# Scores in 384-column matmuls, summed on VectorE, and the attention projection kept in DRAM

## The chip, the cores and the metric

The kernel runs on one core of a Trainium2 chip. The metric is the device time of one execution in microseconds. Engines are called by their names in the profile: PE is TensorE (PEld its weight loads), DVE is VectorE, ACT is ScalarE, POOL is GpSimd, SP is SyncE, which here issues the DMAs.

## What is computed

One decoder block over 2048 positions of width 1024. After an RMSNorm, one projection gives the inputs of two branches and their gates: a convolution branch (gated input, 31 taps per channel, LayerNorm, SiLU) and a sliding-window attention branch. Both are multiplied by a gate, projected, merged by sigmoid gates, projected once more and added to the input; a final RMSNorm follows. The part that the change touches:

```
qb = q.reshape(B, nb, BLOCK, N_KV_HEADS, GROUP, HEAD_DIM)        # BLOCK 128, GROUP 4, HEAD_DIM 64
kb, vb = band(k), band(v)                                        # the block before and this one
scores = einsum("bnqhgd,bnkhd->bnhgqk", qb, kb) * HEAD_DIM ** -0.5
scores = where(in_window & (key_pos >= 0), scores, -1e30)        # WINDOW 128
m = max(max(scores), sink);  p = exp(scores - m)
probs = p / (sum(p) + exp(sink - m));  out = probs @ vb
y_attn = (out * silu(attn_gate)) @ w_attn_out
merged = g_conv * y_conv + g_attn * y_attn
```

All inputs and the output are float32.

## The kernel before

Positions are worked in two sweeps of 1024. Matrices lie with channels on the 128 partitions; a product is made of three matmuls of 512 columns in float32r, high x high, high x low and low x high parts, 24 matmuls for an output tile of 128 channels by 512 positions (a half). A sweep runs through a list of items in a fixed order: queries and keys with their rotation (`mm_q_a`, `mm_q_b`, `mm_ka`, `mm_kb`), values (`mm_v`), the four sets of gates (`mm_ag`, `mm_cg`, `mm_ma`, `mm_mc`), with the convolution's inputs (`mm_gb`, `mm_ga`) strewn between them, then the attention projection (`mm_ya`), the convolution projection (`mm_yc`) and the output projection (`o`).

PE's order is the order of the program. The class `Line` writes that order: it keeps a clock `t` that advances by 0.6825 us per product (`3 * MM_US`, MM_US = 0.2275), and after each product it starts what is due. Background operations (`bg`, among them the convolution's taps, one `scalar_tensor_tensor` of 128x1024 on DVE each, L536) are let out one per `every` microseconds. Chains are generators; a chain's `yield a, b` says that its step took `a` us of PE and that the next step is due `b` us later. Entries of `soon` go out one per product. Operations wrapped in `od(...)` keep the program's order on their engine.

Attention is a chain, one per unit: 8 blocks of 128 queries by 4 key heads in a sweep, 32 units, started every ATT_EVERY = 13.8 us on the line's clock. A unit makes the scores of its four query heads in four groups, each 64 queries of two heads against 192 keys (L799), copies them out of PSUM into the buffer `ss` (ACT L811, DVE L816), takes the maximum with the sink (DVE L819), the exponentials (ACT L822), the reciprocal of the sum (DVE L825) and the scaling (ACT L828). After LAT[0] it transposes the probabilities (`tpp`, L834), splits them (ACT L842, DVE L259), and after LAT[1] multiplies them with the values (`ov`, L858), adds, gates and stores them (ACT L865, DVE L868 and L869, ACT L872, store L881). In a score matmul the 128 partitions hold the high and low parts of a query side by side against the same key rows; `k` has for every 64 keys their high part and their low part (index j), and the two are accumulated in PSUM by two matmuls.

PSUM has three pools: three `mm` banks for halves, three `tp` banks for scores, transposes and values, and one accumulator of two banks for the convolution. `ss` has four buffers, `pt` and `pc` two each. `t2k` is a set of five SBUF buffers of 128x512, used for gates on their way to and from DRAM and by the LayerNorm.

When the last tap is done, the LayerNorm runs as a chain: mean (`lnmu`), centering, variance (`lnvar`, which takes two `mm` banks), `rstd` (ACT L965), then the normalised channels; after that `u_op` multiplies them with their gate into `uT`, which `mm_yc` reads. Results of `mm_ya` are kept in SBUF tiles `mp` (L1053), six of which take the place of convolution results, and are read by L1076 when `mm_yc` gives the other branch's results.

Of the kernel before, what the change touches and what calls it, by code (L numbers as in the profile page):

```python
# [12 lines left out]
F32 = mybir.dt.float32  # L13
# [6 lines left out]
P = 128  # L20
# [9 lines left out]
HD = 64  # L30
# [13 lines left out]
LN_SUB = 2.6  # L44
GLU_AFTER = (0, 6, 12, 16, 19, 22, 25, 28)
ROPE_EVERY = 3.2
CONV_EVERY = 2.4
ATT_EVERY = 13.8
LAT = (19.0, 13.5)
PRIO = 60  # L50
SCALE = HD ** -0.5


@with_exitstack
def hybrid_block(ctx: ExitStack, tc: tile.TileContext, x, xt, par_d, w_in, w_conv, sinks, w_attn, w_out,
# [70 lines left out]
    for u in range(2):  # L126
        us = slice(u * HD, (u + 1) * HD)
        pool.tensor_copy(out=tri[us], in_=causal[us, us])
    tri_i = tri.bitcast(I32).unsqueeze(1).broadcast_to([P, 2, HD])
    eps = const.tile([P, 2], F32, name="eps_t")  # L130
    dve.memset(eps, EPS)
    act.activation(out=eps[:, 1:2], in_=eps[:, 0:1], func=AF.Sqrt)
# [27 lines left out]
    d_q = dram.tile([P, 2, 2, S // HD, 2, P], F32, name="d_q")  # L160
    d_k = dram.tile([P, 2, 2, S // HD, 2, HD], F32, name="d_k")

    d_a = dram.tile([NSWEEP * NKV, P, 2, 2, T], F32, name="d_a")
    d_v = dram.tile([S // P, P, 2, NKV, P], F32, name="d_v")
    v_halo = const.tile([P, NKV, 2, HD], F32R, name="v_halo")
# [82 lines left out]
    def od(op):  # L248

        tc.stamp_issue_order_token(op.ins, "chain")  # L250
        return op
# [261 lines left out]
    def sweep(s):  # L513
# [270 lines left out]
        def attention(n):  # L784
            g, b = divmod(n, NB)
            begun.add(n)
            u = f"{s}_{g}_{b}"
            blk = s * NB + b
            first = blk == 0
            q, k = qk.pop(n)  # L790
            load_qk(n + 1)
            scs = []
            for qh in range(2):
                scs.append(tp_ps.tile([P, 2, 2 * P], F32, tag="tp", name=f"sc{u}_{qh}"))
                c0 = (P - HD * qh) if first else 0
                for hp in range(2):
                    w = q[:, 2 * qh + hp, :]
                    for j in range(2):
                        pe.matmul(out=scs[qh][:, hp, c0:3 * HD], lhsT=w,  # L799
                                  rhs=k[:, qh + c0 // HD:qh + 3, j, :], start=(j == 0), stop=(j == 1))  # L800
            ss = slot(next_of("ss", AT[4:7] + AT[13:14]), [P, 1024], F32, f"ss{u}")
            sx = ss[:, 0:4 * (P + 4)].rearrange("p (h q) -> p h q", q=P + 4)
            sb, ext = sx[:, :, 0:P], sx[:, :, 0:P + 1]
            oT = ss[:, 768:1024].rearrange("p (a q) -> p a q", q=P)
            pool.tensor_copy(out=sx[:, :, P], in_=sink_bc[:, g * GQ:(g + 1) * GQ])
            if first:
                pool.memset(sb, NEG)
            parts = [sb[:, 2 * qh:2 * qh + 2, :] for qh in range(2)]
            for qh, part in enumerate(parts):
                if not first:  # L810
                    od(act.copy(part, scs[qh][:, :, 0:P]))  # L811
                elif qh:
                    od(act.copy(part[:, :, HD:], scs[qh][:, :, HD:P]))
            yield 0.90, 0.8
            for part, sc in zip(parts, scs):
                od(dve.copy_predicated(out=part[:, :, 0:HD], mask=tri_i, data=sc[:, :, P:3 * HD]))  # L816
            st = work.tile([P, 3, GQ], F32, tag="st", name=f"st{u}", bufs=4)
            ngm, den, rinv = (st[:, i, :] for i in range(3))
            od(dve.tensor_reduce(out=ngm, in_=ext, axis=AX.X, op=ALU.max, negate=True))  # L819
            yield 0.0, 1.2  # L820
            for h in range(GQ):
                od(act.activation(out=ext[:, h, :], in_=ext[:, h, :], func=AF.Exp, bias=ngm[:, h:h + 1],  # L822
                                  accum_out=den[:, h:h + 1]))
            yield 0.0, 3.3
            od(dve.reciprocal(out=rinv, in_=den))  # L825
            yield 0.0, 0.6
            for h in range(GQ):
                od(act.activation(out=sb[:, h, :], in_=sb[:, h, :], func=AF.Copy, scale=rinv[:, h:h + 1]))  # L828
            soft.add(n)
            yield 0.0, LAT[0] - 5.9  # L830

            tpp = tp_ps.tile([P, GQ, P], F32, tag="tp", name=f"tpp{u}")
            for h in range(GQ):
                pe.transpose(out=tpp[:, h, :], in_=sb[:, h, :], identity=ident)  # L834
            e2 = slice(s * KC + 2 * g, s * KC + 2 * g + 2)
            qs = slice(b * P, (b + 1) * P)
            pcg = slot(next_of("pc", AT[9:11]), [P, 1024], F32R, f"pc{u}")
            pc, ga = pcg[:, 0:TH], f(pcg[:, TH:TH + 2 * P]).rearrange("p (a q) -> p a q", q=P)
            nc.sync.dma_start(out=ga, in_=spill["ag"][e2, :, qs].rearrange("c p q -> p c q"))
            pt = slot(next_of("pt", AT[7:9]), [P, 2, TH], F32R, f"pt{u}")  # L840
            flat = tpp.rearrange("p h q -> p (h q)")
            od(act.copy(pt[:, 0], flat))  # L842
            yield 0.44, 0.5
            od(split_lo(pt[:, 1], flat, pt[:, 0], dve))
            for a in range(2):
                at = slice(a * HD, (a + 1) * HD)
                pool.affine_select(out=pc[at], in_=f(pt[0:HD, a]), pattern=[[0, 2 * GQ], [1, HD]],  # L847
                                   compare_op=ALU.is_ge, fill=0.0, base=0, channel_multiplier=-1)
            yield 0.0, LAT[1] - 0.5

            ov = tp_ps.tile([P, TH], F32, tag="tp", name=f"ov{u}")
            mix, da, db = (t[:, n // 4 % 2, b % 4, :] for t in vg[0])
            for qh in range(2):
                cols = slice(qh * 2 * P, (qh + 1) * 2 * P)
                seq = [] if first and not qh else [((v_of(g, b - 1), mix)[qh], pt[:, a, cols]) for a in range(2)]
                seq.append(((da, db)[qh], pc[:, cols]))
                for i, (vv, pp) in enumerate(seq):
                    pe.matmul(out=ov[:, cols], lhsT=vv, rhs=pp, start=(i == 0), stop=(i == len(seq) - 1))  # L858
            if n % 4 == 3 and n // 4 + 2 < 2 * NKV:
                line.after(4.0, reload(n // 4 + 2), lambda: True)  # L860
            ovp = ov.rearrange("p (q i r t) -> p i r q t", q=2, i=2, r=2)
            rows = ((slice(0, HD), slice(HD, P)), (slice(HD, P), slice(0, HD)))
            to = [oT[own].rearrange("p i (q t) -> p i q t", t=HD) for own, _ in rows]
            for r in range(2):
                od(act.copy(to[r], ovp[rows[r][1], :, r]))  # L865
            yield 0.72, 0.6
            for r in range(2):
                od(dve.tensor_tensor(out=to[r], in0=ovp[rows[r][0], :, r], in1=to[r], op=ALU.add))  # L868
            od(dve.tensor_tensor(out=oT, in0=oT, in1=ga, op=ALU.mult))  # L869
            yield 0.0, 1.6  # L870
            hl = sb.rearrange("p (l c) q -> p l c q", c=2)
            od(act.copy(hl[:, 0].bitcast(F32R), oT))  # L872
            yield 0.0, 0.5
            od(split_lo(hl[:, 1].bitcast(F32R), oT, hl[:, 0], dve))
            if n == NKV * NB - 1 and s + 1 < NSWEEP:
                pool.tensor_copy(out=v_halo, in_=f(vt[NB // 2 - 1][:, 1]).rearrange(
                    "p g (a d) -> p g a d", d=HD))
            yield 0.0, 1.0

            def store():  # L880
                nc.sync.dma_start(out=d_a[s * NKV + g, :, :, :, qs], in_=hl)  # L881
                done[n] = True

            line.soon.append(store)
# [156 lines left out]
            flat += todo  # L1041


        mp = {}
        mp_tags = [X[2], X[0]] + C[0:6]

        def ya_item(e, first):
            def ev(half, ps):
                if half == 0:
                    if e > 1:  # L1050
                        line.until(lambda: ("u", e - 2, 1) in stored)
                    mp[e] = slot(mp_tags[e], [P, T], F32, f"mp{s}_{e}")
                act.copy(mp[e][:, half * TH:(half + 1) * TH], ps)  # L1053

            prefetch, blocks, _ = project(w_attn[e], lambda k, half: aT[half][k],
                                       f"ya{s}_{e}", ev)
            if not first:
                return prefetch, blocks

            def first_blocks():  # L1060
                start_u()
                if None in aT[0] + aT[1]:
                    line.finish()
                yield from blocks()

            return prefetch, first_blocks
# [4 lines left out]
        def yc_item(e):  # L1071
            def ev(half, ps):
                if not mT:
                    mT.extend(make_tiles(AT, h, f"mT{s}_") for h in range(2))
                ga, g = (load_gate(kind, AF.Sigmoid, e, half) for kind in ("ma", "mc"))
                dve.tensor_tensor(out=ga, in0=mp[e][:, half * TH:(half + 1) * TH], in1=ga, op=ALU.mult)  # L1076
                dve.tensor_tensor(out=g, in0=ps, in1=g, op=ALU.mult)
                pool.tensor_tensor(out=g, in0=g, in1=ga, op=ALU.add)
                put_split(mT[half][e], g, dve)
# [199 lines left out]
```

## Time and profile before

| | us |
|---|---|
| median of the runs (1990.48 to 1991.02) | 1990.72 |
| profiled execution, whole time | 1991.83 |
| its span, first to last instruction | 1990.1 |
| PE busy in the span | 1975.1 |
| DVE busy | 1318.3 |
| ACT busy | 1000.5 |
| POOL busy | 431.8 |

The attention units of the first sweep lie between 210 and 680 us of the span, those of the second between 1197 and 1670; `mm_ya` and `mm_yc` lie from 734 to 911 and from 1722 to 1896. In the rows of groups the columns are: line, engine, operation, written<-read tiles, shapes, count, then busy us, mean ns of one, and the engine's idle time before them with what ended it. In the rows of the timeline: start us, us, engine, line, operation, count, and in brackets the idle time before. In the chain of waits: start us, us, what. In the rows by stretch: the stretch, its length, busy us and count of PE, PEld, DVE, ACT and POOL, the granted clock, the DMA share and GB/s. Rows on waits: who, for whom, total us, times, longest us.

### The profile page before, as it was taken

What the parts mean: (1) busy time and instruction counts of PE and PEld (TensorE: products, weight loads), DVE (VectorE), ACT (ScalarE), POOL (GpSimd) and SP (SyncE); (2) the same over time, 40 slices, a digit from 0 to 9 for tenths busy, and PEclk for the clock granted to TensorE, in tenths of its full rate; (3) what the DMA queues carried; (4) which work ended last, traced back from release to release, by engine and by line L of the source; (5) the groups of instructions that cost most, each with busy time, mean ns of one, the idle gap of its engine ahead of it and who ended that gap; (6) DMA issues with size and microseconds to landing.
All of it is one profiled execution on the core that took longest, in us unless ns stands there. A gap on an engine that the chain in (4) does not pass through costs nothing.

```text
span 1990.1 us, 27077 instructions
## 1 busy us (share of the span) xinstructions
PE 1975.1 (99%) x9256; PEld 1648.4 (83%) x9256; DVE 1318.3 (66%) x1745; ACT 1000.5 (50%) x2270; POOL 431.8 (22%) x462
## 2 busy tenths in 40 slices
PE   8999999999999999999999999999999999999998
PEld 7888888888888878888888888888888888888887
DVE  6998478987887647143858656787787776432424
ACT  7322567556555457344513126776565555553422
POOL 0445323333333332341001121101101110001200
PEclk9999999999999999999999999999999999999999
DMA  8557746665556855456647575555655678553632
GB/s 309 187 185 221 241 156 197 196 194 182 196 192 217 260 184 169 133 195 248 211 134 247 162 240 174 188 184 180 199 181 171 216 228 265 168 189 133 216 123 85
DMA packets 287548, 386.15 MB, mean 194 GB/s; under 512 B 22961, under 2 KB 138033, under 8 KB 287409
## 3 DMA queue, kind: packets, MB, share of 16 engines
q1 hardware_dynamic: 287408, 384.41, 58.8%
q8 instruction: 73, 1.20, 0.2%
q14 instruction: 67, 0.54, 0.1%
HBM read 252.20 MB, written 132.12 MB: 193 GB/s over the span
## 4 chain that ended last, share of the span: by engine, by line
PE 85%; DVE 2%; ACT 1%; issue 1%; DMA 1%; POOL 0%; SPq 0%; DVEq 0%; POOLq 0%; ACTq 0%
PE mm_cg L302 9%; PE mm_ma L302 9%; PE o L1201 9%; PE mm_yc L302 9%; PE mm_ya L302 8%; PE mm_mc L302 8%; PE mm_ga L302 7%; PE mm_gb L302 7%; PE mm_ag L302 7%; PE sc L799 3%; PE mm_q_b L302 2%; PE mm_q_a L302 2%; PE ov L858 2%; PE tpp L834 1%; PE mm_v L302 1%
## 5 line engine op out<-in xcount | busy, mean ns | idle before, releaser
L536 DVE SCALAR_TENSOR_TENSOR acc<-glu,par,acc 128x1024 f32<-128x1024 f32 x464 | 595.5, 1283 | 6.8
L1201 PE MATMUL o<-wo,mT 128*128 128x512 f32 x768 | 174.8, 389 | 0.0
L1201 PEld LDWEIGHTS o<-wo,mT 128*128 128x128 f32 x768 | 144.1, 188 | 30.0
L302 PE MATMUL mm_ya<-aT,whi_ya 128*128 128x512 f32 x512 | 157.9, 389 | 2.2 <-ACT rstd L965 2.2
L302 PE MATMUL mm_cg<-hT,whi_cg 128*128 128x512 f32 x512 | 159.8, 393 | 0.0
L302 PE MATMUL mm_ma<-hT,whi_ma 128*128 128x512 f32 x512 | 159.7, 393 | 0.0
L302 PE MATMUL mm_ag<-hT,whi_ag 128*128 128x512 f32 x512 | 159.5, 393 | 0.0
L302 PE MATMUL mm_mc<-hT,whi_mc 128*128 128x512 f32 x512 | 158.3, 390 | 0.0
L302 PE MATMUL mm_yc<-uT,whi_yc 128*128 128x512 f32 x512 | 157.6, 389 | 0.0
L302 PE MATMUL mm_ga<-hT,whi_ga 128*128 128x512 f32 x448 | 139.4, 392 | 0.0
L302 PE MATMUL mm_gb<-hT,whi_gb 128*128 128x512 f32 x448 | 139.3, 392 | 0.0
L822 ACT ACTIVATE ss<-ss,st 128x129 f32<-128x129 f32 x256 | 100.1, 394 | 65.9 <-DVE st L819 65.6
L847 POOL TENSOR_SCALAR_AFFINE_SELECT pc<-pt 64x512 fp32r<-64x512 f32 x128 | 83.6, 653 | 206.2 <-ACT pt L842 178.5
L302 PEld LDWEIGHTS mm_ya<-aT,whi_ya 128*128 128x128 f32 x512 | 96.0, 188 | 22.5 <-ACT rstd L965 2.6
L302 PEld LDWEIGHTS mm_yc<-uT,whi_yc 128*128 128x128 f32 x512 | 96.1, 188 | 20.0
L302 PEld LDWEIGHTS mm_mc<-hT,whi_mc 128*128 128x128 f32 x512 | 95.4, 188 | 19.7 <-ACT mu L953 0.3
L302 PEld LDWEIGHTS mm_ag<-hT,whi_ag 128*128 128x128 f32 x512 | 93.6, 188 | 17.8
L302 PEld LDWEIGHTS mm_cg<-hT,whi_cg 128*128 128x128 f32 x512 | 93.3, 188 | 17.4
L259 DVE TENSOR_TENSOR pt<-tpp,pt 128x512 fp32r<-128x512 f32 x64 | 44.2, 691 | 95.7 <-ACT pt L842 95.3
L302 PEld LDWEIGHTS mm_ma<-hT,whi_ma 128*128 128x128 f32 x512 | 93.1, 188 | 17.2
L302 PE MATMUL mm_ma<-hT,wlo_ma 128*128 128x512 f32 x256 | 100.0, 391 | 0.0
L302 PE MATMUL mm_cg<-hT,wlo_cg 128*128 128x512 f32 x256 | 100.0, 390 | 0.0
(452 smaller groups left out, 4274.5 us busy)
## 6 DMA issues: line engine op xcount, KB each, us to landing
qk<-d_q SPq DMA_DIRECT2D x64, 256.0 KB, 4.3
d_a<-ss SPq DMA_DIRECT2D x64, 256.0 KB, 2.8
aT<-d_a SPq DMA_DIRECT2D x32, 512.0 KB, 5.6
qk<-d_k SPq DMA_DIRECT2D x60, 256.0 KB, 4.5
d_k<-hlk SPq DMA_DIRECT2D x16, 512.0 KB, 4.6
d_q<-hq_c SPq DMA_DIRECT2D x16, 512.0 KB, 4.6
raw_ag<-in_w_in_dram SPq DMA_DIRECT2D x32, 256.0 KB, 4.2
d_ag<-ag SPq DMA_DIRECT2D x32, 256.0 KB, 2.9
```

Source lines behind the costliest of these rows:

```text
L259: return eng.tensor_tensor(out=out_, in0=full, in1=f(hi), op=ALU.subtract)
L302: pe.matmul(out=ps, lhsT=a, rhs=b, start=(k == 0 and i == 0), stop=(k == KC - 1 and i == 2))
L536: od(dve.scalar_tensor_tensor(out=to, in0=glu[c][:, j:j + T], scalar=tap(c, j), in1=acc[c], op0=ALU.mult, op1=ALU.add))
L799: pe.matmul(out=scs[qh][:, hp, c0:3 * HD], lhsT=w, rhs=k[:, qh + c0 // HD:qh + 3, j, :], start=(j == 0), stop=(j == 1))
L822: od(act.activation(out=ext[:, h, :], in_=ext[:, h, :], func=AF.Exp, bias=ngm[:, h:h + 1], accum_out=den[:, h:h + 1]))
L834: pe.transpose(out=tpp[:, h, :], in_=sb[:, h, :], identity=ident)
L847: pool.affine_select(out=pc[at], in_=f(pt[0:HD, a]), pattern=[[0, 2 * GQ], [1, HD]], compare_op=ALU.is_ge, fill=0.0, base=0, channel_multi ...
L858: pe.matmul(out=ov[:, cols], lhsT=vv, rhs=pp, start=(i == 0), stop=(i == len(seq) - 1))
L1201: pe.matmul(out=ps, lhsT=a[:, c0:c0 + P], rhs=r, start=(k == 0 and i == 0), stop=(k == KC - 1 and i == 2))
```

## The change

The two matmuls that accumulated a group's scores against the high and the low keys become one matmul of 2 x 192 columns, whose two halves lie side by side in one bank. ACT copies the low half into the score buffer, DVE adds the high half to it, and the mask is applied from that buffer. A unit's scores are made in two steps, the second about SCORE_GAP after the first. The sink's column moves to the front of the buffer. Delays of the line change (CONV_EVERY, LAT[1], the waits around the softmax). Results of the attention projection go into a `t2k` buffer and from there to DRAM (`d_mp`); they are loaded again for L1076, and the evacuation no longer asks for a `u` to have been issued.

```
--- before.py
+++ after.py
@@ -44,11 +44,13 @@
 LN_SUB = 2.6
 GLU_AFTER = (0, 6, 12, 16, 19, 22, 25, 28)
 ROPE_EVERY = 3.2
-CONV_EVERY = 2.4
+CONV_EVERY = 2.5
 ATT_EVERY = 13.8
-LAT = (19.0, 13.5)
+LAT = (19.0, 18.5)
+SCORE_GAP = 3.2
 PRIO = 60
 SCALE = HD ** -0.5
+SW = 1 + 3 * HD
 
 
 @with_exitstack
@@ -126,7 +128,7 @@
     for u in range(2):
         us = slice(u * HD, (u + 1) * HD)
         pool.tensor_copy(out=tri[us], in_=causal[us, us])
-    tri_i = tri.bitcast(I32).unsqueeze(1).broadcast_to([P, 2, HD])
+    tri_i = tri.bitcast(I32).unsqueeze(1).broadcast_to([P, GQ, HD])
     eps = const.tile([P, 2], F32, name="eps_t")
     dve.memset(eps, EPS)
     act.activation(out=eps[:, 1:2], in_=eps[:, 0:1], func=AF.Sqrt)
@@ -160,6 +162,7 @@
     d_q = dram.tile([P, 2, 2, S // HD, 2, P], F32, name="d_q")
     d_k = dram.tile([P, 2, 2, S // HD, 2, HD], F32, name="d_k")
 
+    d_mp = dram.tile([NSWEEP * KC, P, T], F32, name="d_mp")
     d_a = dram.tile([NSWEEP * NKV, P, 2, 2, T], F32, name="d_a")
     d_v = dram.tile([S // P, P, 2, NKV, P], F32, name="d_v")
     v_halo = const.tile([P, NKV, 2, HD], F32R, name="v_halo")
@@ -789,35 +792,36 @@
             first = blk == 0
             q, k = qk.pop(n)
             load_qk(n + 1)
-            scs = []
-            for qh in range(2):
-                scs.append(tp_ps.tile([P, 2, 2 * P], F32, tag="tp", name=f"sc{u}_{qh}"))
-                c0 = (P - HD * qh) if first else 0
-                for hp in range(2):
-                    w = q[:, 2 * qh + hp, :]
-                    for j in range(2):
-                        pe.matmul(out=scs[qh][:, hp, c0:3 * HD], lhsT=w,
-                                  rhs=k[:, qh + c0 // HD:qh + 3, j, :], start=(j == 0), stop=(j == 1))
             ss = slot(next_of("ss", AT[4:7] + AT[13:14]), [P, 1024], F32, f"ss{u}")
-            sx = ss[:, 0:4 * (P + 4)].rearrange("p (h q) -> p h q", q=P + 4)
-            sb, ext = sx[:, :, 0:P], sx[:, :, 0:P + 1]
+            sx = ss[:, 0:GQ * SW].rearrange("p (h q) -> p h q", q=SW)
+            ext, sb = sx[:, :, 0:P + 1], sx[:, :, 1:P + 1]
             oT = ss[:, 768:1024].rearrange("p (a q) -> p a q", q=P)
-            pool.tensor_copy(out=sx[:, :, P], in_=sink_bc[:, g * GQ:(g + 1) * GQ])
+            pool.tensor_copy(out=sx[:, :, 0], in_=sink_bc[:, g * GQ:(g + 1) * GQ])
             if first:
                 pool.memset(sb, NEG)
-            parts = [sb[:, 2 * qh:2 * qh + 2, :] for qh in range(2)]
-            for qh, part in enumerate(parts):
-                if not first:
-                    od(act.copy(part, scs[qh][:, :, 0:P]))
-                elif qh:
-                    od(act.copy(part[:, :, HD:], scs[qh][:, :, HD:P]))
-            yield 0.90, 0.8
-            for part, sc in zip(parts, scs):
-                od(dve.copy_predicated(out=part[:, :, 0:HD], mask=tri_i, data=sc[:, :, P:3 * HD]))
+            for qh in range(2):
+                c0 = (P - HD * qh) if first else 0
+                banks = []
+                for hp in range(2):
+                    sc = tp_ps.tile([P, 4, P], F32, tag="tp", name=f"sc{u}_{qh}{hp}")
+                    sc = sc.rearrange("p a b -> p (a b)").rearrange("p (j c) -> p j c", j=2)
+                    pe.matmul(out=sc[:, :, c0:3 * HD].rearrange("p j (b t) -> p j b t", t=HD),
+                              lhsT=q[:, 2 * qh + hp, :],
+                              rhs=k[:, qh + c0 // HD:qh + 3].rearrange("p b j t -> p j b t"),
+                              start=True, stop=True)
+                    banks.append(sc)
+                to = [sx[:, 2 * qh + hp, 1 + c0:1 + 3 * HD] for hp in range(2)]
+                for part, sc in zip(to, banks):
+                    od(act.copy(part, sc[:, 1, c0:3 * HD]))
+                yield 0.35, 0.5
+                for part, sc in zip(to, banks):
+                    od(dve.tensor_tensor(out=part, in0=sc[:, 0, c0:3 * HD], in1=part, op=ALU.add))
+                yield 0.0, 0.0 if qh else SCORE_GAP - 0.85
+            od(dve.copy_predicated(out=sb[:, :, 0:HD], mask=tri_i, data=sx[:, :, P + 1:]))
             st = work.tile([P, 3, GQ], F32, tag="st", name=f"st{u}", bufs=4)
             ngm, den, rinv = (st[:, i, :] for i in range(3))
             od(dve.tensor_reduce(out=ngm, in_=ext, axis=AX.X, op=ALU.max, negate=True))
-            yield 0.0, 1.2
+            yield 0.0, 2.6
             for h in range(GQ):
                 od(act.activation(out=ext[:, h, :], in_=ext[:, h, :], func=AF.Exp, bias=ngm[:, h:h + 1],
                                   accum_out=den[:, h:h + 1]))
@@ -827,7 +831,7 @@
             for h in range(GQ):
                 od(act.activation(out=sb[:, h, :], in_=sb[:, h, :], func=AF.Copy, scale=rinv[:, h:h + 1]))
             soft.add(n)
-            yield 0.0, LAT[0] - 5.9
+            yield 0.0, LAT[0] - SCORE_GAP - 7.35
 
             tpp = tp_ps.tile([P, GQ, P], F32, tag="tp", name=f"tpp{u}")
             for h in range(GQ):
@@ -1041,16 +1045,13 @@
             flat += todo
 
 
-        mp = {}
-        mp_tags = [X[2], X[0]] + C[0:6]
 
         def ya_item(e, first):
             def ev(half, ps):
-                if half == 0:
-                    if e > 1:
-                        line.until(lambda: ("u", e - 2, 1) in stored)
-                    mp[e] = slot(mp_tags[e], [P, T], F32, f"mp{s}_{e}")
-                act.copy(mp[e][:, half * TH:(half + 1) * TH], ps)
+                m = t2k(f"mp{s}_{e}_{half}")
+                act.copy(m, ps)
+                line.soon.append(lambda: nc.sync.dma_start(
+                    out=d_mp[s * KC + e, :, half * TH:(half + 1) * TH], in_=m))
 
             prefetch, blocks, _ = project(w_attn[e], lambda k, half: aT[half][k],
                                        f"ya{s}_{e}", ev)
@@ -1073,7 +1074,9 @@
                 if not mT:
                     mT.extend(make_tiles(AT, h, f"mT{s}_") for h in range(2))
                 ga, g = (load_gate(kind, AF.Sigmoid, e, half) for kind in ("ma", "mc"))
-                dve.tensor_tensor(out=ga, in0=mp[e][:, half * TH:(half + 1) * TH], in1=ga, op=ALU.mult)
+                m = t2k(f"lmp{s}_{e}_{half}")
+                nc.sync.dma_start(out=m, in_=d_mp[s * KC + e, :, half * TH:(half + 1) * TH])
+                dve.tensor_tensor(out=ga, in0=m, in1=ga, op=ALU.mult)
                 dve.tensor_tensor(out=g, in0=ps, in1=g, op=ALU.mult)
                 pool.tensor_tensor(out=g, in0=g, in1=ga, op=ALU.add)
                 put_split(mT[half][e], g, dve)
```

## The prediction

> **What bounds the kernel now.** I read the page first (span, busy shares), then who PE waited for, then the chain of waits in two places.
>
> ```profile
> span 1990.1 us, 27077 instructions
> PE 1975.1 (99%) x9256; PEld 1648.4 (83%) x9256; DVE 1318.3 (66%) x1745; ACT 1000.5 (50%) x2270; POOL 431.8 (22%) x462
> PE mm_gb L302 <- ACT u_c L377: 5.5, 1, 5.5
> PE mm_ya L302 <- ACT rstd L965: 2.2, 1, 2.2
> PE mm_q_b L302 <- DVE ra_q__0_1573 L614: 0.4, 1, 0.4
> PE sc L799 <- DVE pt L259: 0.2, 1, 0.2
> ```
>
> PE is busy through 99% of the span, and its four listed waits add up to 8.3 us, 5.5 of them at the start, which the change doesn't touch. So time is won by a shorter matmul stream, and lost where PE, whose order is fixed by hand, meets an operand or a PSUM bank that isn't ready. What a matmul costs is its place in that stream:
>
> ```profile
> 187.35 10.88 PE mm_ag L302 x48
> 209.79 0.84 PE sc L799 x8
> 1224.91 0.87 PE sc L799 x8
> 1232.63 0.44 PE tpp L834 x4
> 1235.14 0.71 PE ov L858 x6
> ```
>
> A 512-column matmul takes 10.88/48 = 0.2267 us, one of 256 columns (ov) 0.71/6 = 0.118, one of 128 (tpp) 0.110, and one of 192 (sc) 0.87/8 = 0.109. Below about 256 columns the price no longer falls: a score matmul of 192 columns pays for almost 256.
>
> **1. Eight score matmuls become four of 384 columns.** On the line from 256 to 512 columns, 384 take 0.172 us; four take 0.69 instead of 0.87, so 0.18 us per unit. For 60 units that is 10.8 us. The four units at the sequence's start (0.84 us now) go to two of 128 and two of 256 columns, 0.46 us: 1.5 us more. Together **-12.3 us**, all on PE, hence on the path. Bounds: the operand is read in six pieces of 64 columns, and no row has such a read above the floor. At worst 384 columns cost two of 192 (0.218) and only the 1.5 us stay. I take 0.172, since the 192-column read, already in three pieces, is no dearer than the contiguous 128.
> [...]
>
> **2. More evacuation, on engines that are not the bound.**
>
> ```profile
> L868 DVE TENSOR_TENSOR ss<-ov,ss 64x256 f32<-64x256 f32 x128 | 53.9, 421 | 63.0 <-ACT ss L865 59.1 <-PE mm_gb L302 2.5
> L259 DVE TENSOR_TENSOR pt<-tpp,pt 128x512 fp32r<-128x512 f32 x64 | 44.2, 691 | 95.7 <-ACT pt L842 95.3
> L816 DVE COPY_PREDICATED ss<-tri,sc 128x128 f32<-128x128 int32 x128 | 33.0, 298 | 23.7 <-PE sc L799 10.8 <-ACT ss L811 9.9 <-ACT ss L813 1.4
> L536 DVE SCALAR_TENSOR_TENSOR acc<-glu,par,acc 128x1024 f32<-128x1024 f32 x464 | 595.5, 1283 | 6.8
> L811 ACT COPY ss<-sc 128x256 f32<-128x256 f32 x120 | 43.2, 373 | 45.3 <-PE sc L799 41.8 <-DMA wlo_ma<-d_lo 0.4
> L842 ACT CAST pt<-tpp 128x512 fp32r<-128x512 f32 x64 | 37.4, 585 | 32.9 <-PE tpp L834 32.5
> 230.00:650.00 420.00, 419.77 (x2111) 354.96 (x2110) 338.58 (x456) 256.29 (x690) 145.03 (x172) 1.00 0.60 191
> 1190.00:1640.00 450.00, 450.00 (x2257) 380.68 (x2257) 345.96 (x475) 279.06 (x731) 60.73 (x100) 1.00 0.60 192
> ```
>
> DVE: an addition of 192 columns lies on the line through 256 (421 ns) and 512 (691): 353 ns. Four additions and one predicated copy of 256 elements (about 433, from 298 at 128 and the same slope) are 1.85 us, where two predicated copies took 0.60: +1.25 us a unit. A tap of the convolution every 2.5 instead of 2.4 us gives back 0.23 taps of 1283 ns, 0.29 us. Net +0.96 us in the 13.7 us of a unit, 7 points: DVE goes from 338.58/420 = 81% to 88% in the first sweep's attention, from 77% to 84% in the second's. ACT: four copies of 192 columns (320 ns on the line from 373 to 585) for two of 256: +0.53 us, 61% to 65%. Neither becomes the bound by its sum; what it costs is delay, next.
>
> **3. Banks: six a unit instead of four, on three.** The tp banks serve the scores, the transposes (tpp) and the values (ov). In the new order the fourth score matmul reuses the bank of the first, so PE waits there until the first addition is done. The line's clock advances 0.6825 us per product (three matmuls of MM_US) and starts a step at the first product past its due time: additions are issued 1.03 us after the unit begins (0.35 + 0.68), the second pair of matmuls at 3.76 (0.35 + five products). So the first addition must end 3.9 us after the unit's start. Today's predicated copy is issued at 2.27 (0.90 + two products). When does DVE get there?
>
> ```profile
> 264.27 1.03 PE L799 MATMUL sc<-qk 128*128 128x192 f32 x8
> 268.93 0.49 DVE L816 COPY_PREDICATED ss<-tri,sc 128x128 f32<-128x128 int32 x2
> 319.69 1.00 PE L799 MATMUL sc<-qk 128*128 128x64 f32 x8
> 325.97 0.50 DVE L816 COPY_PREDICATED ss<-tri,sc 128x128 f32<-128x128 int32 x2
> 361.64 0.81 PE L799 MATMUL sc<-qk 128*128 128x192 f32 x6
> 366.75 0.50 DVE L816 COPY_PREDICATED ss<-tri,sc 128x128 f32<-128x128 int32 x2
> 1224.75 1.03 PE L799 MATMUL sc<-qk 128*128 128x192 f32 x8
> 1226.27 0.49 DVE L816 COPY_PREDICATED ss<-tri,sc 128x128 f32<-128x128 int32 x2
> ```
>
> In the ordinary unit (1224.75) DVE starts 1.52 us after the matmuls: a first addition would end near 1.9 at the latest, two microseconds early. But for some nine units of the first sweep (264 to 375) DVE is 4.66, 6.28 and 5.11 us late. The addition stands 1.24 us earlier in DVE's order, which is half a tap, 0.64 us; with its own 0.35 it ends at 4.37, 5.99 and 4.82, that is 0.44, 2.06 and 0.89 us past the 3.9. A PE wait delays all that follows, so a steady lag is paid once: 2 us is the low end. Paid anew by each of nine units at the mean of the first and last, 0.67, it is 6, and with the 0.96 us of part 2 making the lag grow again up to 12. I take **+5 us**, the nearer end being 6, and nothing in the second sweep, where units have two microseconds.
>
> **4. Longer latencies.** The maximum over the scores is issued 4.79 us into the unit instead of 2.27; the waits up to tpp sum to 19.0 us instead of 19.9, so the softmax loses some 3 us of cover and tpp keeps its place. LAT[1] then adds 5 us up to ov: a unit holds its score buffer, one of four, about 4 us longer.
>
> ```profile
> 1267.85 0.52 SPq L881 DMA_DIRECT2D d_a<-ss  x1
> d_a<-ss SPq DMA_DIRECT2D x64, 256.0 KB, 2.8
> 1280.90 0.70 ACT L811 COPY ss<-sc 128x256 f32<-128x256 f32 x2
> ```
>
> The unit of 1224.75 stores at 1267.85, lands at about 1270.7, and its buffer is written by the fourth unit after at 1280.90: 10 us of cover, 6 left. Zero. If that goes, ACT's copy comes late and adds to part 3.
>
> **5. The convolution ends later.** From 210 us to the end of the taps near 676 there are some 195 of them at 2.4 us; 0.1 us more each puts the LayerNorm about 20 us back, in each sweep.
>
> ```profile
> 737.21 0.63 PE L920 MATMUL lnvar<-vsump,ones 128*128 128x512 f32 x2
> 741.33 1.27 ACT L965 ACTIVATE rstd<-lnvar,eps_t 128x512 f32<-128x512 f32 x2
> L259 DVE TENSOR_TENSOR uT<-lcg,uT x16: 676/684/1786, 762.5 to 791.1; 128x512 fp32r<-128x512 f32 x16
> 823.96 87.04 PE mm_yc L302 x384
> 1714.45 0.47 PE lnvar L920 x2
> 1722.44 87.04 PE mm_ya L302 x384
> ```
>
> On today's clock uT would be done near 811 and is first read at 823.96: covered by 12 us. lnvar takes two of the three mm banks; today that costs the 2.2 us of the second wait above, because ACT came 4.1 us late. In the second sweep it moves from before mm_ya (1714.45) into it. Between 0 and 4.1 us in each sweep, 2.2 in all today: I take no change, by that nearest row; the ends are a gain of 2.2 and a loss of 6.
>
> **6. Projection through DRAM.** The evacuation (ACT, L1053) stays, into a t2k buffer; 32 stores and 32 loads of 256 KB come onto SP's queue, and L1076 waits for one more load. The wait of the evacuation for u goes, and was no PE wait.
>
> ```profile
> SPq L596 <- POOL lmc L1078: 20.6, 13, 4.8
> lma<-d_ma SPq DMA_DIRECT2D x32, 256.0 KB, 3.3
> 856.64 0.69 DVE L1077 TENSOR_TENSOR lmc<-mm_yc,lmc 128x512 f32<-128x512 f32 x1 [0.96 <-PE mm_yc L302]
> 862.08 0.69 DVE L1077 TENSOR_TENSOR lmc<-mm_yc,lmc 128x512 f32<-128x512 f32 x1 [0.20 <-PE mm_yc L302]
> ```
>
> A half of mm_yc takes 5.44 us and uses three of the five t2k buffers instead of two. Already now the gate loads wait for buffers (first line). The third load goes out when L1076 has freed its buffer of the half before: 0.69 + 3.3 = 4.0 us a half, under 5.44, so DVE still waits for PE. The new stores stand on SP until ACT's copy is done, as those of the gates do; queued behind a blocked load or store are the weights' loads, a block (10.9 us) ahead. Zero: even a loop of 6 us would lose 0.56 x 16 = 9 us a sweep, inside the two spare mm banks. POOL's copy of the sinks only changes its column.
>
> **Sum.** 1990.1 - 12.3 + 5 = 1982.8 us of span. The profiled execution took 1991.83 in all, 1.73 outside its span and 1.1 over the runs' median of 1990.72; the same -7.3 on that median is **1983 us**.
>
> **Rivals.**
> - No wait worth naming: DVE's lag in those nine units comes from today's spacing (tpp and ov side by side), which LAT spreads out. 1990.7 - 12.3 = 1978.4. For it: the second sweep, no unit late. Chance 0.25.
> - Slower: the bank of the first score. If DVE, at 88%, lags through the first sweep as it does in the nine units, 32 waits of 0.67 cost 21 us: 2000. It decides once the mean wait over 64 units passes 0.19 us, the gain per unit. Against it: 12% of DVE still free, and PE waited 0.2 us for such a bank so far. Chance 0.15. [...]
> - mm banks: lnvar inside mm_ya in both sweeps, 4.1 us each less today's 2.2: 1983 + 6 = 1989, the same. Chance 0.11.
> - 384 columns at 0.218: the change does nothing for PE. 1990.7 - 1.5 + 5 = 1994. Against it: the 512-column price. Chance 0.07.
>
> **How the numbers follow.** The forecast (1979.5 to 1986.5 by its waits of 2 to 8 us) has 0.42. Anything within 0.2% (4 us) can't be told from no change. Faster: 0.42 + 0.25 = 0.67; same: 0.11, most of the fourth rival and a milder bank wait, 0.17; slower 0.16. The range runs from just below the case without waits, 1977, to past the fourth rival, 1995, and leaves out most of the bank rival.
>
> **What would show it.** sc: 256 matmuls, four in 0.69 us of chain. PE's waits: the second pair of scores on DVE's addition, a few microseconds, between 264 and 375 us only. DVE near 88% and 84% in the attention stages. lnvar about 15 us later on the clock. L1077 still waiting for mm_yc. Wrong if sc waits in both sweeps, if four scores take 0.87, or if mm_ya or mm_yc waits for t2k evacuations.

## The result, and the profile after

The changed kernel took 2010.03 us (median; 2009.11 to 2014.66), the kernel before 1990.87 on the same chip: a ratio of 1.0099, interval 1.0081 to 1.0116. It is slower by 1%; the forecast was 1983, the range 1977 to 1995. The profiled execution took 2014.66 in all, some 5 us over the other three, with a span of 2013.0; the stages below are those of that execution, so they show 22.9 us of loss in the span where the medians show 19.2.

First the page of the changed kernel and its list of PE's waits. The change moves line numbers: L1079, L1080 and L1081 are now the two multiplications and the addition of `mm_yc` (L1076 to L1078 before), L1078 the new load, L808 the scores, L818 the new addition, L262 the split of results on DVE, L599 the loads of gates.

```profile
span 2013.0 us, 26940 instructions
PE 1975.2 (98%) x9000; PEld 1637.7 (81%) x9000; DVE 1375.4 (68%) x1937; ACT 1019.6 (51%) x2396; POOL 430.2 (21%) x462
```
```profile
PE mm_yc L305 <- DVE lmc L1080: 12.4, 6, 4.0
PE o L1204 <- ACT wo L1149: 6.6, 3, 4.1
PE mm_gb L305 <- ACT u_c L380: 5.9, 1, 5.9
PE mm_ga L305 <- ACT glu L562: 2.2, 1, 2.2
PE o L1204 <- DVE lmc L1080: 1.8, 1, 1.8
PE o L1204 <- DVE wo L262: 1.1, 3, 0.6
PE sc L808 <- DVE ss L818: 0.3, 1, 0.3
```

The waits that the forecast looked for are missing: 0.3 us for a bank of the scores, none for `lnvar`. In their place stand 21.9 us in `mm_yc` and `o` (12.4 + 6.6 + 1.8 + 1.1), two stages that the change hardly seems to touch. The stages, from the first matmul of one to the first of the next (of `o`: to its last matmul), read off PE's timelines, differences taken before rounding; the last column is an experiment below that keeps the new scores and nothing else that costs:

| us | before | after | after - before | scores alone, taps at 2.4 |
|---|---|---|---|---|
| `mm_ag` to `mm_ya`, first sweep | 546.6 | 540.8 | -5.8 | 542.3 |
| `mm_ya` | 90.0 | 87.6 | -2.4 | 88.6 |
| `mm_yc` | 87.0 | 100.4 | +13.3 | 87.0 |
| `o` | 87.8 | 93.7 | +5.9 | 87.8 |
| `mm_ag` to `mm_ya`, second sweep | 525.7 | 522.2 | -3.5 | 520.4 |
| `mm_ya` | 87.0 | 87.6 | +0.5 | 87.2 |
| `mm_yc` | 87.0 | 93.0 | +6.0 | 87.0 |
| `o` | 86.8 | 95.0 | +8.2 | 86.8 |

So the stages with attention gained 9.3 us, and the two projections behind it lost 33.4.

**Where the 33 us go.** One step of the loop in `mm_yc`, from the timelines of all engines (start, length, engine, line, operation; in brackets the idle time before and what ended it):

```profile
864.94 0.68 DVE L1080 TENSOR_TENSOR lmc<-mm_yc,lmc 128x512 f32<-128x512 f32 x1
865.05 0.32 SPq L1078 DMA_DIRECT2D lmp<-d_mp  x1
868.88 1.69 DVE L1079 TENSOR_TENSOR lma<-lmp,lma 128x512 f32<-128x512 f32 x1 [3.26 <-DMA lmp<-d_mp]
870.50 0.68 DVE L262 TENSOR_TENSOR mT<-lmc,mT 128x512 fp32r<-128x512 f32 x1
871.20 0.32 SPq L1078 DMA_DIRECT2D lmp<-d_mp  x1
875.73 0.98 DVE L1079 TENSOR_TENSOR lma<-lmp,lma 128x512 f32<-128x512 f32 x1 [4.56 <-DMA lmp<-d_mp]
876.64 0.68 DVE L1080 TENSOR_TENSOR lmc<-mm_yc,lmc 128x512 f32<-128x512 f32 x1
877.47 0.70 PE L305 MATMUL mm_yc<-uT,whi_yc 128*128 128x512 f32 x2 [3.98 <-DVE lmc L1080]
```

Read it upwards. PE waits 3.98 us for a PSUM bank, which L1080 frees. L1080 waits for nothing of its own; it stands behind L1079 of the next half in DVE's order, and L1079 waits 4.56 us for the new load. That load was issued at 871.20, the moment L262 (870.50, 0.68 long) had let go of its `t2k` buffer, and that L262 had stood behind the previous L1079, which had waited 3.26 us for the previous load. So each load waits for a split, each split for a multiplication, each multiplication for a load: the load's latency (3.6 us from issue to landing, the median of the 32) lies in series with the work, although DVE is idle. All 16 halves, before and after, from the rows of the line (count, ns, first and last start):

```profile
L1077 DVE TENSOR_TENSOR lmc<-mm_yc,lmc x16: 679/691/692, 829.4 to 914.6; 128x512 f32<-128x512 f32 x16
```
```profile
L1080 DVE TENSOR_TENSOR lmc<-mm_yc,lmc x16: 676/684/686, 826.8 to 925.5; 128x512 f32<-128x512 f32 x16
L1080 DVE TENSOR_TENSOR lmc<-mm_yc,lmc x16: 683/684/686, 1825.6 to 1921.7; 128x512 f32<-128x512 f32 x16
```

Before: (914.6 - 829.4)/15 = 5.68 us a half, near PE's 5.44. After: 6.58 in the first sweep and 6.41 in the second. SP's own waits between 820 and 920 us name the buffers; the loads of the other operands, queued behind, pay too:

```profile
SPq L599 <- DMA lmp<-d_mp: 19.1, 12, 2.9
SPq L599 <- POOL lmc L1081: 17.7, 14, 2.0
SPq L599 <- DVE lma L1079: 12.4, 13, 1.8
SPq L1078 <- DVE mT L262: 7.0, 11, 1.5
```

**What the projections lose besides the waits.** Stretches just behind two of the long waits (busy us of PE, PEld, DVE, ACT, POOL, then the granted clock):

```profile
877.50:881.50 4.00, 4.00 (x12) 3.15 (x13) 1.29 (x2) 1.25 (x2) 1.95 (x2) 0.64 0.72 228
1921.20:1925.20 4.00, 4.00 (x9) 2.89 (x10) 1.90 (x4) 0.62 (x1) 1.28 (x1) 0.50 1.02 417
```

With the clock at 0.50, 4 us hold 9 matmuls instead of 18 (0.2267 us each). In the `mm_yc` and `o` stages 30 matmuls start about 0.427 us after the one before instead of 0.227: 30 x 0.2 = 6.0 us, on top of 25.1 us that 15 matmuls lost by starting more than half a microsecond after the one before. With the two waits of about 4 us (4.0 and 4.1) the clock fell to 0.50, from 878.60 to 882.01 us and from 1919.67 to 1926.49, but it also did with shorter ones: from 926.39 to 929.80 with one of 2.2 us, and from 1899.19 to 1902.60 with one of 2.8; the last section comes back to this.

**Scores and engines.** What the forecast had said of these, from the groups of the changed kernel, its rows by stretch, and the one wait for a score bank in the timelines:

```profile
L818 DVE TENSOR_TENSOR ss<-sc,ss 128x192 f32<-128x192 f32 x240 | 74.3, 352 | 24.7 <-ACT ss L815 23.2
L815 ACT COPY ss<-sc 128x192 f32<-128x192 f32 x240 | 65.1, 322 | 55.0 <-PE sc L808 50.5 <-issue 2.0 <-POOL ss L799 1.1
L820 DVE COPY_PREDICATED ss<-tri,ss 128x256 f32<-128x256 int32 x64 | 36.3, 567 | 2.0
```
```profile
230.00:650.00 420.00, 419.64 (x2010) 351.82 (x2010) 360.16 (x540) 270.21 (x757) 150.22 (x175) 1.00 0.60 191
1190.00:1640.00 450.00, 447.77 (x2137) 376.10 (x2136) 359.24 (x544) 280.51 (x773) 60.11 (x100) 1.00 0.62 194
```
```profile
347.39 0.51 PE L808 MATMUL sc<-qk 128*128 128x384 f32 x2
351.70 0.62 DVE L818 TENSOR_TENSOR ss<-sc,ss 128x192 f32<-128x192 f32 x2
352.12 0.44 PE L808 MATMUL sc<-qk 128*128 128x384 f32 x1 [0.35 <-DVE ss L818]
```

### The profile page after: what moved, and what is told of

It reads as the page before. It is cut to its first block, busy times and chain, and to the rows that moved or that the text cites. A ratio compares the mean times of both kernels' runs of the same rounds, so it can differ in the third digit from the quotient of the medians.

```text
span 2013.0 us, 26940 instructions
## 1 busy us (share of the span) xinstructions
PE 1975.2 (98%) x9000; PEld 1637.7 (81%) x9000; DVE 1375.4 (68%) x1937; ACT 1019.6 (51%) x2396; POOL 430.2 (21%) x462
## 5 line engine op out<-in xcount | busy, mean ns | idle before, releaser
L1204 PE MATMUL o<-wo,mT 128*128 128x512 f32 x768 | 181.2, 397 | 9.5 <-ACT wo L1149 6.6
L305 PE MATMUL mm_yc<-uT,whi_yc 128*128 128x512 f32 x512 | 160.6, 395 | 12.4 <-DVE lmc L1080 12.4
L872 DVE TENSOR_TENSOR ss<-ov,ss 64x256 f32<-64x256 f32 x128 | 54.0, 422 | 101.5 <-ACT ss L869 94.4
L305 PEld LDWEIGHTS mm_cg<-hT,whi_cg 128*128 128x128 f32 x512 | 94.0, 188 | 16.7
L818 DVE TENSOR_TENSOR ss<-sc,ss 128x192 f32<-128x192 f32 (+2 forms) x256 | 77.7, 345 | 38.8 <-ACT ss L815 37.3
L1079 DVE TENSOR_TENSOR lma<-lmp,lma 128x512 f32<-128x512 f32 x32 | 24.4, 763 | 114.5 <-DMA lmp<-d_mp 69.6
```

The lines of the kernel that those rows point to most:

```text
L305: pe.matmul(out=ps, lhsT=a, rhs=b, start=(k == 0 and i == 0), stop=(k == KC - 1 and i == 2))
L818: od(dve.tensor_tensor(out=part, in0=sc[:, 0, c0:3 * HD], in1=part, op=ALU.add))
L1079: dve.tensor_tensor(out=ga, in0=m, in1=ga, op=ALU.mult)
L1204: pe.matmul(out=ps, lhsT=a[:, c0:c0 + P], rhs=r, start=(k == 0 and i == 0), stop=(k == KC - 1 and i == 2))
```

## The experiments

The theory after the traces: the score matmuls bring their gain, and the projection's way through DRAM (the detour) costs more than that, by the loop over the shared buffers. Rival: the late LayerNorm, or the longer attention, puts everything behind it late.

| kernel | median us | ratio to before | interval |
|---|---|---|---|
| 1 scores without the detour | 1998.22 | 1.0034 | 1.0022 to 1.0046 |
| 2 detour alone | 2019.53 | 1.0139 | 1.0124 to 1.0154 |
| 3 own buffers for the loads | 1987.99 | 0.9984 | 0.9974 to 0.9993 |
| 4 bank freed first | 1992.20 | 1.0006 | 0.9996 to 1.0015 |
| 5 as 3, taps at 2.4 | 1983.33 | 0.9953 | 0.9938 to 0.9968 |
| 6 as 1, taps at 2.4 | 1981.54 | 0.9940 | 0.9924 to 0.9957 |
| 7 before, taps at 2.5 | 1998.36 | 1.0029 | 1.0019 to 1.0040 |
| 8 as 3 and 4, taps at 2.4 | 1986.02 | 0.9967 | 0.9957 to 0.9978 |
| 9 whole change, taps at 2.4 | 2005.37 | 1.0069 | 1.0052 to 1.0086 |
| 10 whole change, six buffers | 2005.15 | 1.0068 | 1.0053 to 1.0083 |

The kernel before had medians of 1991.03 to 1991.69 beside them.

**1. The scores without the detour.** The changed kernel with `mp` kept in SBUF as before:

```
-                m = t2k(f"mp{s}_{e}_{half}")
-                act.copy(m, ps)
-                line.soon.append(lambda: nc.sync.dma_start(out=d_mp[...], in_=m))
+                if half == 0:
+                    if e > 1:
+                        line.until(lambda: ("u", e - 2, 1) in stored)
+                    mp[e] = slot(mp_tags[e], [P, T], F32, f"mp{s}_{e}")
+                act.copy(mp[e][:, half * TH:(half + 1) * TH], ps)
...
-                m = t2k(f"lmp{s}_{e}_{half}")
-                nc.sync.dma_start(out=m, in_=d_mp[...])
-                dve.tensor_tensor(out=ga, in0=m, in1=ga, op=ALU.mult)
+                dve.tensor_tensor(out=ga, in0=mp[e][:, half * TH:(half + 1) * TH], in1=ga, op=ALU.mult)
```

> The changed kernel with the projection's results kept in SBUF as before; scores, delays and taps stay changed. Theory (t2k buffers): the whole loss lies in mm_yc and o, so this loses the loss and keeps the gain of the scores: 1990.9 - 12.3 - 2 = about 1977 us, mm_yc 87 us in both sweeps. Rival (late LayerNorm: uT ready only when mm_yc begins): the delays are still there, so mm_yc stays long and the time stays over 2000 us. Rival (scores cost more than they give): 1995 us or more.

Missed by 21 us: 1998.22, in the range of the rival by which the scores cost more than they give. `mm_yc` and `o` were clean, but `mm_ya` was not. PE's waits, and the ACT timeline at the larger one:

```profile
PE mm_ya L305 <- ACT mp L1058: 11.4, 2, 8.3
```
```profile
764.59 9.19 ACT L949 ACTIVATE cv<-cv,par 128x1024 f32<-128x1024 f32 x8 [2.48 <-DVE cv L948]
773.68 1.12 ACT L343 CAST uT<-lcg 128x512 fp32r<-128x512 f32 x2
774.70 1.06 ACT L1058 COPY mp<-mm_ya 128x512 f32<-128x512 f32 x2
```

The copy that frees the `mm` bank stands on ACT behind 9.19 us of the LayerNorm's work and the first `uT`, because `line.until` lets those out ahead of it: `mp` from its third tile on takes the place of convolution results that `u` must have read. With taps every 2.5 us that work comes only now. That would be a second cost of the change, which the detour hides: the changed kernel has no such wait.

**2. The detour alone.** The kernel before with the two pieces of the diff that write and read `d_mp`, nothing else.

> The kernel before with only the projection through DRAM. Theory (t2k buffers): mm_yc grows to 93 to 98 us and o to 94 us in each sweep, together 25 to 33 us, so 2015 to 2024 us. Rival (late LayerNorm): it is early here, so no loss, about 1991 us. Rival (traffic or SP's queue): also slow, 2015 us; the next kernel tells it from the theory.

2019.53, inside: +28.5 us against the 1991.03 beside it, with the LayerNorm early and the old scores. The loss needs neither. Its loop ran at (930.1 - 830.2)/15 = 6.66 us a half.

**3. Own buffers for the loads.** In the changed kernel:

```
-                m = t2k(f"lmp{s}_{e}_{half}")
+                m = slot(next_of("lmp", [X[2], X[0]]), [P, TH], F32, f"lmp{s}_{e}_{half}")
```

> The changed kernel, but the 32 loads of the projection go to two SBUF buffers of their own (X[2] and X[0]) instead of t2k; loads, stores, bytes and PE's order are the same. Theory (t2k buffers): with 2 t2k buffers a half as before, PE's waits in mm_yc go: about 1977 us. Rival (traffic, SP's queue or the load's latency): the loads are as many and as late, PE's waits stay, 2005 us or more. Rival (late LayerNorm): over 2000 us.

1987.99: 22.0 us of the changed kernel's 2010.03 gone, with the same traffic and the same order on DVE, though not all that the scores promise. The loads now go out ahead of the multiplication's turn, and L1079 waits for its gate instead (timeline of DVE), at (913.5 - 826.2)/15 = 5.82 us a half; PE's waits in the two stages shrink to 3.0 us, here two of the four rows:

```profile
871.65 0.32 SPq L1078 DMA_DIRECT2D lmp<-d_mp  x1
877.24 0.69 DVE L1079 TENSOR_TENSOR lma<-lmp,lma 128x512 f32<-128x512 f32 x1 [4.42 <-ACT lma L600]
```
```profile
L1080 DVE TENSOR_TENSOR lmc<-mm_yc,lmc x16: 678/684/686, 826.2 to 913.5; 128x512 f32<-128x512 f32 x16
```
```profile
PE mm_yc L305 <- DVE lmc L1080: 0.5, 1, 0.5
PE o L1204 <- ACT wo L1149: 0.8, 1, 0.8
```

**4. The bank freed first.** The changed kernel with its five shared buffers, the two multiplications exchanged and their order kept:

```
-                dve.tensor_tensor(out=ga, in0=m, in1=ga, op=ALU.mult)
-                dve.tensor_tensor(out=g, in0=ps, in1=g, op=ALU.mult)
+                od(dve.tensor_tensor(out=g, in0=ps, in1=g, op=ALU.mult))
+                od(dve.tensor_tensor(out=ga, in0=m, in1=ga, op=ALU.mult))
```

> The changed kernel with the two multiplications of a half swapped and held in the program's order on DVE: the one that frees the mm bank goes ahead of the one that needs the reloaded projection; buffers and loads as in the changed kernel. Theory in its sharper form (DVE's order: the bank waits behind a multiplication that waits for a load): PE's waits in mm_yc go, since the loop load to load is 4 us a half: about 1978 us. Theory in its plain form (five buffers can't carry three loads a half, in whatever order): a half still takes 7 us, 2005 us. Rival (late LayerNorm or traffic): over 2000 us.

1992.20: 17.8 us gone without a single buffer more, though 14 us above the sharper form and well under the plain one. `mm_yc` took 87.1 and 87.0 us, so the bank no longer waits. But the halves of the first sweep still went at (916.4 - 826.0)/15 = 6.03 us, and the lag came out in its `o`: 99.2 us, 11.4 more than before, with these waits and a granted clock of 0.63 from 908 to 912 us and 0.50 from 916 to 920; the second sweep's `o` lost nothing.

```profile
PE o L1204 <- ACT wo L1149: 3.7, 4, 1.4
```

The order on DVE was the other half of the loop. Together 3 and 4 say that either link, cut alone, undoes most of it.

**5, 6, 7, 8. The LayerNorm's time.** One number, in kernel 3, kernel 1 and the kernel before (there the other way), and in kernel 3 with the order of 4:

```
-CONV_EVERY = 2.5
+CONV_EVERY = 2.4
```

> The changed kernel with own buffers for the loads (1988.0 us) and the convolution's taps every 2.4 us again, so that the LayerNorm starts some 20 us earlier. Theory (the two losses are separate: the buffer loop, taken away here, and the late LayerNorm, which lets the first gate loads of mm_yc out only at 819 us and so makes the first wo tiles late): the 5.3 us that the o stage of the first sweep lost at 900 to 920 us shrink to under 1, 1981 to 1984 us. Rival (three loads a half fill the DMA, the LayerNorm has nothing to do with it): 1987 to 1990.

1983.33, 4.7 us below kernel 3 and inside the theory's range, but not by the theory's way: the first sweep's `o` still takes 92.7 us, 4.9 more than before. Part of the gain is the wait of 2.2 us for `glu` near 1520 us, which all kernels with the new scores and late taps have and none with early taps; why was not tried.

> The score change alone (the projection kept in SBUF as before; 1998.2 us with a tap every 2.5 us), with taps every 2.4 us. Theory (the 11.4 us for which PE waited for the evacuation of mm_ya came from the late LayerNorm, whose work stood ahead of those copies on ACT and DVE): the waits go, 1978 to 1984 us. Rival (the longer attention itself makes them late, whatever the taps' spacing): 1994 to 1999.

1981.54, inside: 16.7 of the 21 us that kernel 1 was over its expectation hung on that one number. The longest of PE's waits of this kernel beyond the start:

```profile
PE mm_ya L305 <- ACT rstd L969: 0.7, 1, 0.7
PE sc L808 <- DVE ss L818: 0.6, 2, 0.3
PE sc L808 <- DVE ss L872: 0.5, 1, 0.5
```

It is the fastest kernel of the study, 10 us under the one before: the new scores without the detour and without the later LayerNorm.

> The kernel before with nothing changed but the taps' spacing, 2.5 us for 2.4. Theory (a late LayerNorm collides with the evacuations of mm_ya that stay in SBUF): PE waits for those copies 8 to 14 us in all, 2000 to 2007 us. Rival (it needs the new scores): 1990 to 1993.

1998.36: slower by 7 us, a little below the range that was given, because PE waited once and not twice (6.7 us for the same copy, and 1.7 us of half clock behind it: granted 0.50 from 779.5 to 783.0 us, 8 matmuls in 3.5 us). The later LayerNorm costs by itself, without the new scores.

```profile
PE mm_ya L302 <- ACT mp L1053: 6.7, 1, 6.7
```

> The changed kernel with all three: own buffers for the loads, the multiplication that frees the bank first on DVE, taps every 2.4 us. Theory: nothing is left but the shorter matmul stream, 1978 to 1982 us, as or a little below the kernel with own buffers and early taps. Rival (the order on DVE makes the gate buffers come free later, and the DMA is the limit): 1986 to 1992.

1986.02, above the theory's range and at the edge of the rival's. It isn't below kernel 5: the order adds nothing once the buffers are apart. That it costs 3 us, by the rival's way or any other, was not shown: the runs of the two overlap (1981.65 to 1986.00 and 1984.55 to 1988.44), the two profiled spans are 1984.3 and 1984.0, and the halves went at 5.85 us here, (912.9 - 825.1)/15, and at 6.02 in kernel 5.

**9. The whole change with the LayerNorm early.**

> The whole change with one number back: taps every 2.4 us, the loads still in the five shared buffers. Theory (the loop over the shared buffers costs its time whenever the LayerNorm ends; the late LayerNorm added 4.7 us to the kernel with own buffers): 2003 to 2008 us, PE's waits for the gating product and for wo staying near 20 us. Rival (the loop bites only because the late LayerNorm lets no gate load run ahead): under 1992.

2005.37, as the theory had it: 4.7 us better, and the loop stays (8.5 us of waits for L1080 in `mm_yc`, 5.4 for `wo`, 16.7 in the two stages where near 20 were said).

**10. Six shared buffers.**

```
-        return work.tile([P, TH], dt, tag="t2k", name=name, bufs=5)
+        return work.tile([P, TH], dt, tag="t2k", name=name, bufs=6)
```

> The whole change with six shared buffers instead of five, so that two halves of three loads fit. Theory (the loop is one buffer short: with six, the load of the next half needs a buffer of the half before the present one): most of the 22 us that own buffers took away go, 1987 to 1994 us, and PE waits under 3 us for the gating product. Rival (it is the traffic of the third load, or any shared pool keeps the load behind SP's order): 2003 to 2012.

2005.15: only 5 us better, the theory missed, the rival's range hit. The loop changed one link and stayed a loop. Second sweep, all engines, and the row of the line:

```profile
1851.66 0.68 DVE L1080 TENSOR_TENSOR lmc<-mm_yc,lmc 128x512 f32<-128x512 f32 x1
1852.48 1.29 POOL L1081 TENSOR_TENSOR lmc<-lmc,lma 128x512 f32<-128x512 f32 x1 [4.21 <-DVE lmc L1080]
1853.79 0.32 SPq L1078 DMA_DIRECT2D lmp<-d_mp  x1
1858.13 0.69 DVE L1079 TENSOR_TENSOR lma<-lmp,lma 128x512 f32<-128x512 f32 x1 [2.98 <-DMA lmp<-d_mp]
```
```profile
L1080 DVE TENSOR_TENSOR lmc<-mm_yc,lmc x16: 683/684/686, 1820.7 to 1914.0; 128x512 f32<-128x512 f32 x16
```

L1080 is no longer behind the next L1079, but the load now leaves 0.02 us after POOL's addition of the half before: (1914.0 - 1820.7)/15 = 6.22 us a half. PE waited only 2.7 us for the gating product in `mm_yc`, under 3 as the theory said; the lag was handed on to `o`, whose `wo` tiles came late (5.9 us); the mean granted clock of this execution was 0.996, that of the kernel before 0.999. So six buffers for five do not open the loop while the load shares a rotation with the results that wait for it. Kernel 3 has seven in all, five and two, and a shared set of seven was not run, so there the number and the separation are not told apart; kernel 4 shows that the number need not change.

**The three parts against each other** (medians of this study; old scores, detour and late taps together were not run):

| us | in SBUF, 2.4 | in SBUF, 2.5 | through DRAM, 2.4 | through DRAM, 2.5 |
|---|---|---|---|---|
| old scores | 1990.9 | 1998.4 | 2019.5 | - |
| new scores | 1981.5 | 1998.2 | 2005.4 | 2010.0 |

The scores are worth -9.4 and -14.1 us with early taps, and nothing with late taps in SBUF: there `mm_ya` starts 6.6 us sooner (727.5 for 734.1) and `lnvar` only 3.2 (754.7 for 757.9), so PE waits longer for the copies (11.4 us for 6.7), and the 2.2 us for `glu` come on top. The detour costs 28.6 and 23.9 us with early taps, 11.8 with late ones, where it also takes away the wait of `mm_ya`.

## Why the prediction was wrong

**Part 1, right.** In the chain of waits of kernel 6 a pair of score matmuls is one step:

```profile
1193.29 0.35 PE sc L808 x2
```

Two pairs a unit are 0.70 us, 0.69 foretold, and the whole -12.3 came out as about -11: summing in each trace by how much a matmul started later than is usual for its kind and its predecessor's (delays above 40 ns) gives 14.0 us before, 47.9 after and 16.2 in kernel 6; the spans less these are 1976.1, 1965.1 and 1964.6. One matmul is 0.35/2 = 0.175 us, near the 0.172 taken from the rows.

**Part 2, right in kind.** The addition took 352 ns (353 said), the copy 322 (320), the predicated copy 567, not 433. DVE came to 360.16/420 = 86% and 80% where 88 and 84 were said, ACT to 64%.

**Part 3, right in place, wrong in size.** PE did wait for the first addition inside the stretch named, at 352.12, for 0.35 us, not 5. In nine units between 264 and 376 us the first addition began 2.4 us after its matmul on the average (the latest, this one, 4.31), where 4.02 to 5.64 had been taken. The step stands earlier in DVE's order, for which half a tap was given, and LAT now spreads `tpp` and `ov`, as the rival without a wait said; which of the two was worth more than was thought, no run tells apart. That rival was right about this term.

**Part 4, right as to PE.** PE waited for no score buffer. ACT did, behind POOL, which sets the sink's column and waits for the buffer's store (162.2 us in all, 269.7 before): two of its copies came 0.78 and 0.36 us late by that, and no wait of PE shows behind them.

**Part 5, right in the times, wrong in the price.** `lnvar` moved from 737.2 to 758.6, and the last `uT` began at 815.5 where 811 was said. Of the 12 us of cover none was left, since `mm_yc` began at 816.2 and not at 823.96; PE did not wait for `uT` even so. But the danger was looked for in the `mm` banks that `lnvar` takes, and it lay mainly in the copies that `line.until` holds behind `u`: by the medians the later taps cost 7.5 us with the old scores in SBUF (kernel 7) and 16.7 with the new ones (kernel 1 against 6). In the changed kernel itself the wait for those copies was taken away by the very detour; there the later taps cost 4.7, for which part 5 had put nothing.

**Part 6 is the step that failed.** It read "The third load goes out when L1076 has freed its buffer of the half before: 0.69 + 3.3 = 4.0 us a half, under 5.44, so DVE still waits for PE", and priced the detour at zero. The load goes out when a split (L262) has freed one, behind the addition on POOL, the cast on ACT and another load's multiplication: 6.58 us a half. The quoted wait of SP for POOL's L1078, 20.6 us, had shown that buffers are freed there and not by the multiplication. Nor did the spare banks cover it, as "even a loop of 6 us would lose 0.56 x 16 = 9 us a sweep" had it. At 5.82 us (kernel 3, first sweep) `mm_yc` lost only 0.9 us, but its last product was taken up 10.2 us after its last matmul had ended (3.6 before), and `o`, which has its own tiles to get ready by the same queues, lost 5.5; at 6.22 (kernel 10, second sweep) the lag was 11.3 us, and the two stages lost 3.6 and 6.7. The sum fails by this term: 0 for 24 to 29 us. Two smaller misses, nothing for the later taps (4.7) and +5 for the banks (4.7 too much), cancelled by luck.

No rival held it, though "wrong if mm_ya or mm_yc waits for t2k evacuations" stood among the signs; it was given no price, and so no place in the range.

**Open.** Why the first sweep's `o` still loses 4.9 us in kernel 5, when the second sweep loses nothing, was not settled; the trace shows `wo` and `mT` late (PE's waits 1.6 + 0.5 and 1.2 us), and the halves of `mm_yc` at 6.02 us in the first sweep and 5.58 in the second.

## What to carry to other kernels

When a load is given a buffer from a rotation that the results of the same step pass through, ask which operation last held that buffer and write out the loop load, multiplication, next release, load: if the latency of a transfer is in it and its period is longer than PE's step (here 6.58 against 5.44 us), that period sets the pace, whatever the engines' shares say. Cut it with a buffer outside that rotation, or by putting the operation that frees a PSUM bank ahead of the one that waits for the load. And when one number moves a whole chain later, look for copies whose place in an engine's order depends on that chain.

## What the runs showed of the hardware that was not expected

In these traces the half clock did not follow the length of a single wait. In the detour alone (kernel 2) a wait of 3.7 us was followed at once by full clock, while one of 2.0 us, with no other in the 90 us before it, stood ahead of seven slow matmuls. Rows by stretch of kernel 2, around the end of the long wait and then around the short one, and of the changed kernel up to the end of its wait of 4 us:

```profile
879.50:882.91 3.41, 1.57 (x7) 1.34 (x8) 1.69 (x2) 0.27 (x1) 1.83 (x2) 1.00 0.34 108
882.91:886.33 3.42, 3.42 (x17) 2.81 (x16) 1.29 (x2) 1.37 (x3) 1.28 (x1) 1.00 0.79 256
1889.85:1893.26 3.41, 1.53 (x7) 0.99 (x6) 1.29 (x2) 0.83 (x2) 0.45 (x1) 1.00 0.44 156
1893.26:1896.67 3.41, 3.41 (x10) 2.64 (x9) 1.29 (x2) 1.25 (x2) 1.30 (x2) 0.50 0.83 259
```
```profile
875.18:878.60 3.42, 1.14 (x5) 1.00 (x6) 1.58 (x2) 0.00 (x0) 2.14 (x2) 1.00 0.32 119
```

The stretches are cut where steps of 3.41 us begin and end. In each of the nine traces where the granted clock changes between 250 and 1965 us, all its changes lie on one grid of 3.41 us, and it stays at half for whole steps of that grid; in the changed kernel's trace these are the steps from 878.60, 926.39, 1899.19, 1919.67 and 1923.08 us. The long wait fell across two steps and left PE busy for 1.69 us of the one and 1.57 of the other; the short one left 1.53 us of its step. Over these traces, all 15 steps at full clock in which PE was busy for less than 0.44 of the step were followed by half clock, 6 of 17 between 0.44 and 0.60, and none above. The four of the changed kernel had 0.33, 0.36, 0.25 and 0.24, and none of them was empty: its waits of about 4 us left 1.14 us busy (the last row) and 0.82. So in these traces half clock came behind steps with a small share of PE, and a wait of 2.0 us cost it where one of 3.7, split between two steps, did not; what decides it was not shown. The border is an estimate, since the ends of matmuls are modelled.
